# Row softmax on one core: nine load tiles beginning with 13 rows instead of ten beginning with 3 and 5, and every early load on one queue

## The chip, the core and the metric

The kernel runs on one core of a Trainium2 chip. The metric is the device time of one execution in microseconds (us); lower is better. The kernel before was run ten times; the median of those runs is 159.91 us, the lowest 159.77 and the highest 168.56.

## The reference

The input is `x` of shape 16 x 1024 x 512 in fp32, that is, 16,384 rows of 512 numbers. Each row is divided by a temperature of 2 and put through a softmax:

```python
def reference(x):
    x_scaled = x / 2.0
    x_max = np.max(x_scaled, axis=-1, keepdims=True)
    exp_x = np.exp(x_scaled - x_max)
    return (exp_x / np.sum(exp_x, axis=-1, keepdims=True)).astype(np.float32)
```

The input has 33.55 MB and so has the output. Both cross between the main memory (HBM) and the core's own memory (SBUF) once, 67.11 MB in all.

## The kernel before, in words

**Rows.** With 128 partitions, the 16,384 rows make 128 rows for each partition. From here on a "row" is one such step: 128 x 512 numbers, 256 KB, 2 KB in each partition. The kernel takes the exponential of `0.5 * x` without subtracting the maximum. At the end it looks whether all row sums lie in a safe interval, and has a slow general version of the computation (`rounds`) that runs only if they don't. With this input it is skipped.

**Tiles.** `TILES` lists the transfers: how many rows each one moves, and at which row of the buffer `arena` it stands. A tile is one load and, later, one store. In partition p, the rows of a tile lie one after the other both in HBM and in SBUF, so a tile of 15 rows is 128 runs of 30,720 bytes. The buffer has 98 rows (`ARENA`). The first 98 rows of the input are loaded without waiting for anything; the last two tiles, of 15 rows each, are loaded over tiles that have already been stored. `LATE` says which stores each of the two has to wait for.

**Queues.** `early()` issues the first loads ahead of the barrier with which the program begins: tile 0 on SP's queue and tile 1 on ScalarE's. `loads()` issues tiles 2 to 7 on ScalarE's queue (six loads of 15 rows), before ScalarE computes anything. GpSimd issues the two late loads, after the first `TURN` rows (83) have had their exponentials. SP issues all the stores, in the order of the tiles, each as soon as the tile's last multiplication has ended. `SPREAD` names the one tile whose load is cut in three: all rows but the last for 128 partitions, the last row for partitions 0 to 125, and the last row for partitions 126 and 127.

**ScalarE** (ACT, lines L204 and L271) takes one row at a time: an exponential in place, with the row's sum on the side in `stats`. A chunk is 3 rows first (`HEAD`), then always 5 rows (`E`). Before each chunk it waits until the tile that holds it has landed as a whole. TensorE's queue does that waiting: it waits for each tile's `ld` semaphore and then grants that tile's chunks through `s_go` (L140 is the place where ScalarE takes a grant).

**VectorE** (DVE, lines L166 and L169) takes up to three chunks of a tile at a time: a reciprocal of the sums, and one multiplication of up to 15 rows by them. In the last tile it takes one chunk at a time.

The order of the instructions on each engine is written out by hand; no scheduler moves them.

Of the kernel before, what the change touches and what calls it, by code (L numbers as in the profile page):

```python
# [7 lines left out]


TILES = [  # L10
    (3, 0), (5, 3), (15, 8), (15, 23), (15, 38), (15, 53), (15, 68), (15, 83), (15, 0), (15, 15),
]

LATE = {8: (0, 1, 2), 9: (3,)}
ARENA = 98

HEAD = [3]
E = 5

SPREAD = 1  # L20

TURN = 83

LO, HI = 1.0, 1.0e30
G = 64
# [3 lines left out]
def kernel(  # L29
# [5 lines left out]
    nc = tc.nc  # L35
# [24 lines left out]
    tiles, base = [], 0  # L60
# [5 lines left out]
    def dram(ap, t):  # L66
        b, r, _ = tiles[t]
        return ap[b * P : (b + r) * P].rearrange("(p r) d -> p r d", r=r)

    def sb(t):  # L70
        _, r, at = tiles[t]
        return arena[:, at : at + r, :]
# [8 lines left out]

    pairs = []
    for k, t in enumerate(owner):
        most = 1 if t == len(tiles) - 1 else 3
        if pairs and len(pairs[-1]) < most and owner[pairs[-1][0]] == t:
            pairs[-1].append(k)
        else:
            pairs.append([k])
    upto = [1 + max(j for j, ks in enumerate(pairs) if owner[ks[0]] == t) for t in range(len(tiles))]

    ld = [nc.alloc_semaphore(f"ld{t}") for t in range(len(tiles))]
    s_home = {t: nc.alloc_semaphore(f"s_home{t}") for t in LATE}
    s_near = nc.alloc_semaphore("s_near")
# [19 lines left out]
    def load(eng, t):  # L113
        r = tiles[t][1]
        parts = [(0, P, 0, r)]
        if t == SPREAD:
            parts = [(0, P, 0, r - 1), (0, 126, r - 1, r), (126, P, r - 1, r)]
        for p, q, lo, hi in parts:
            eng.dma_start(  # L119
                out=sb(t)[p:q, lo:hi], in_=dram(xf, t)[p:q, lo:hi]  # L120
            ).then_inc(ld[t], 16)

    stored_by = {u: s_home[t] for t, us in LATE.items() for u in us}
    for t, (_, r, at) in enumerate(tiles):
        over = {u for u, (_, ru, au) in enumerate(tiles[:t]) if at < au + ru and au < at + r}
        assert over <= {u for v, us in LATE.items() if v <= t for u in us}

    def landings(ts):
        return 16 * len(list(ts))
# [21 lines left out]
            eng.reg_add(i, i, 1)  # L151

    def early():
        load(nc.sync, 0)
        load(nc.scalar, 1)

    def loads():
        for t in range(2, min(LATE)):
            load(nc.scalar, t)

    def program():
# [13 lines left out]
        nc.gpsimd.memset(ones[:, :], 1.0).then_inc(s_ones, 1)  # L175
        nc.gpsimd.wait_ge(s_exp, starts.index(TURN))
        for t, us in LATE.items():
            nc.gpsimd.wait_ge(s_home[t], landings(us))
# [14 lines left out]
        for t in range(len(tiles)):  # L193
            nc.tensor.wait_ge(ld[t], 48 if t == SPREAD else 16).then_inc(s_go, owner.count(t))
        nc.tensor.wait_ge(s_ones, 1)
# [85 lines left out]
    entry.instructions = []  # L281
    nc.switch_bb("main", None)
    early()
    first = list(entry.instructions)
    at = next(k for k, i in enumerate(head) if type(i).__name__ == "InstDrain")
    entry.instructions = head[:at] + first + head[at:]
    act = []
    entry.instructions = list(entry.instructions) + [i for i in jumps if i not in act]
    nc.switch_body(here, parent=None, valid_engines=[i.engine for i in jumps])
    loads()  # L290
    program()

# [29 lines left out]
```

## Time and profile before

| | before |
|---|---|
| median of ten runs | 159.91 us |
| the profiled execution: its time | 160.02 us |
| the profiled execution: its span, first to last instruction | 158.7 us |
| outside the span in that execution | 1.3 us |
| VectorE busy | 73.2 us, 46% |
| ScalarE busy | 80.6 us, 51% |
| DMA engines, all queues together | 99.0% of 16 engines' span |
| bytes moved | 67.11 MB, 423 GB/s over the span |
| DMA packets | 3024 |

The span is cut into 40 slices of 3.97 us on the profile's page. The row "DMA" gives how busy the core's 16 DMA engines were in each slice, in tenths. The part on DMA queues gives the share of the 16 engines' span that each queue's packets took: q1 is SP's queue (all stores, and the load of tile 0), q10 is ScalarE's (the loads of tiles 1 to 7) and q0 is GpSimd's (the two late loads). A packet here is the run of one tile in one partition: of 30,720 bytes for a tile of 15 rows. With each DMA go 16 tiny packets that raise its semaphore.

### The profile page before, as it was taken

How to read it: one execution, taken by the hardware profiler on the slowest of the kernel's cores; microseconds unless marked ns; L12 is line 12 of the kernel's file. 1: busy time of each engine (PE TensorE's matmuls, PEld its weight loads, DVE VectorE, ACT ScalarE, POOL GpSimd, SP SyncE). 2: the span in 40 equal slices, each digit the busy share in tenths (PEclk: the TensorE clock that was granted, in tenths of full speed). 3: DMA queues.
4: the chain of work that ended last, by engine and by line, in shares of the span. 5: the costliest groups of instructions: out<-in, count | busy, mean ns of one | idle time of the engine just before them, and what ended most of it. 6: DMA issues, size and time to landing. Idle time of an engine off the chain costs nothing. (4 is left out here: it accounts for less than half of the span.)

```text
span 158.7 us, 657 instructions
## 1 busy us (share of the span) xinstructions
PE 0.2 (0%) x2; PEld 0.1 (0%) x2; DVE 73.2 (46%) x27; ACT 80.6 (51%) x257; POOL 2.2 (1%) x8
## 2 busy tenths in 40 slices
PE   0000000000000000000000000000000000000000
PEld 0000000000000000000000000000000000000000
DVE  0047001992981990059500991008922990993000
ACT  0590598696498009940399001991597009940000
POOL 0000000000000000000000300000000000010000
DMA  7999998989899999999999999999999998989895
GB/s 266 386 496 397 463 414 340 511 354 514 387 472 395 472 395 465 403 465 403 457 410 457 410 449 418 441 426 441 426 418 449 418 449 387 480 387 480 387 472 256
DMA packets 3024, 67.11 MB, mean 423 GB/s; under 512 B 336, under 2 KB 336, under 8 KB 720
## 3 DMA queue, kind: packets, MB, share of 16 engines
q1 hardware_dynamic: 1584, 34.34, 50.5%
q10 hardware_dynamic: 1152, 24.90, 37.0%
q0 software_dynamic: 288, 7.86, 11.5%
HBM read 33.55 MB, written 33.55 MB: 423 GB/s over the span
## 5 line engine op out<-in xcount | busy, mean ns | idle before, releaser
L271 ACT ACTIVATE arena<-arena x125 | 76.6, 614 | 54.3 <-ACTq L140 54.3
L169 DVE TENSOR_TENSOR arena<-arena,recip 128x7680 f32<-128x7680 f32 (+2 forms) x12 | 70.2, 5847 | 0.4
L166 DVE RECIPROCAL recip<-stats 128x15 f32<-128x15 f32 (+2 forms) x12 | 2.7, 224 | 70.4 <-ACT arena L271 61.4
L271 ACT ACTIVATION_READ_ACCUMULATOR arena<-arena x125 | 23.4, 187 | 0.0
L200 ACT ACT_TABLE_LOAD x1 | 1.3, 1283 | 5.7 <-issue 5.7
L119 POOL DMA_DIRECT2D arena<-in_x_dram x2 | 1.3, 638 | 84.8 <-ACT arena L271 84.8
L204 ACT ACTIVATE arena<-arena 128x512 f32<-128x512 f32 x3 | 1.9, 618 | 0.0
L180 POOL TENSOR_SCALAR inside<-stats 128x128 f32<-128x128 f32 x1 | 0.6, 631 | 51.8 <-ACT arena L271 51.8
L204 ACT ACTIVATION_READ_ACCUMULATOR arena<-arena 128x1 f32 x3 | 0.6, 186 | 0.0
L196 PE MATMUL total<-ones,count 128*1 128x1 f32 x2 | 0.2, 164 | 143.9 <-DVE inside L184 143.9
L184 DVE SCALAR_TENSOR_TENSOR inside<-inside,stats 128x128 f32<-128x128 f32 x1 | 0.3, 285 | 0.0
L188 DVE TENSOR_SCALAR flag<-total 1x1 int32<-1x1 f32 x1 | 0.1, 147 | 0.3 <-PE total L196 0.3
L196 PEld LDWEIGHTS total<-ones,count 128*1 128x1 f32 x2 | 0.1, 80 | 143.9 <-DVE inside L184 143.9
L175 POOL MEMSET ones<- 128x1 f32 x1 | 0.1, 99 | 2.2 <-POOLq L37 2.2
L306 POOL MEMSET const-float32-0.0<- 128x1 f32 x1 | 0.1, 105 | 0.2 <-issue 0.2
L306 POOL MEMSET const-bfloat16-1.0<- 128x1 bf16 x1 | 0.1, 108 | 0.0
L306 POOL MEMSET const-uint8-127<- 128x1 uint8 x1 | 0.1, 107 | 0.0
L306 POOL MEMSET const-float32-1.0<- 128x1 f32 x1 | 0.1, 105 | 0.0
L184 DVE DVE_READ_ACCUMULATOR inside<-inside,stats 128x1 f32 x1 | 0.1, 83 | 0.0
## 6 DMA issues: line engine op xcount, KB each, us to landing
out_dram<-arena SPq DMA_DIRECT2D x8, 3840.0 KB, 26.3
arena<-in_x_dram ACTq DMA_DIRECT2D x6, 3840.0 KB, 46.7
arena<-in_x_dram POOLq DMA_DIRECT2D x2, 3840.0 KB, 33.7
out_dram<-arena SPq DMA_DIRECT2D x1, 1280.0 KB, 22.8
arena<-in_x_dram ACTq DMA_DIRECT2D x1, 1024.0 KB
arena<-in_x_dram SPq DMA_DIRECT2D x1, 768.0 KB, 5.6
out_dram<-arena SPq DMA_DIRECT2D x1, 768.0 KB, 14.7
arena<-in_x_dram ACTq DMA_DIRECT2D x1, 252.0 KB
```

Of the source, the lines that this page charges most:

```text
L119: eng.dma_start(out=sb(t)[p:q, lo:hi], in_=dram(xf, t)[p:q, lo:hi]).then_inc(ld[t], 16)
L166: nc.vector.reciprocal(out=recip[:, b : b + c], in_=stats[:, b : b + c])._wait_ge(s_exp, ks[-1] + 1).then_inc(s_rec, 1)
L169: nc.vector.tensor_mul(out=arena[:, a : a + c], in0=arena[:, a : a + c], in1=recip[:, b : b + c].unsqueeze(2).to_broadcast([P, c, D]),)._w ...
L175: nc.gpsimd.memset(ones[:, :], 1.0).then_inc(s_ones, 1)
L180: nc.gpsimd.tensor_scalar(out=inside[:, :], in0=stats[:, :], scalar1=LO, scalar2=HI, op0=Alu.max, op1=Alu.min,)._wait_ge(s_exp, len(sizes) ...
L184: nc.vector.scalar_tensor_tensor(out=inside[:, :], in0=inside[:, :], scalar=1.0, in1=stats[:, :], op0=Alu.mult, op1=Alu.is_equal, accum_ou ...
L188: nc.vector.tensor_scalar(out=flag[:, :], in0=total[:, :], scalar1=float(N), scalar2=None, op0=Alu.is_ge,)._wait_ge(s_tot, 1).then_inc(s_f ...
L196: nc.tensor.matmul(total[:, :], lhsT=count[:, :], rhs=ones[:, :], start=True, stop=True)._wait_ge(s_cnt, 2).then_inc(s_tot, 1)
L200: nc.scalar.preload_act_table(Exp)
L204: ins = nc.scalar.activation(out=arena[:, b], in_=arena[:, b], func=Exp, scale=0.5, accum_out=stats[:, b : b + 1],)
L271: ins = nc.scalar.activation(out=data, in_=data, func=Exp, scale=0.5, accum_out=stats[:, r : n_rows - E + 1 + r][:, bass.ds(now, 1)],)
L306: nc = _bacc.Bacc("TRN2", target_bir_lowering=False, num_devices=1)
```

## The change

The list of tiles begins with one of 13 rows where there were one of 3 and one of 5; five of 15 follow, then one of 10, and the two late ones of 15 as before. There are nine tiles for ten. The buffer is filled by the first seven: 13 + 5 x 15 + 10 = 98. The first late tile now lies over tiles 0 and 1, the second over tile 2. The load of tile 0 is the one cut in three (12 rows, then the thirteenth in two pieces), and it is issued by ScalarE; SP issues no load any more. GpSimd waits for 78 rows' exponentials, no longer for 83. VectorE takes one chunk at a time in tile 0 too, so that it multiplies 3, 5 and 5 rows there. The chunks of ScalarE stay as they were.

```diff
 TILES = [
-    (3, 0), (5, 3), (15, 8), (15, 23), (15, 38), (15, 53), (15, 68), (15, 83), (15, 0), (15, 15),
+    (13, 0), (15, 13), (15, 28), (15, 43), (15, 58), (15, 73), (10, 88), (15, 0), (15, 15),
 ]
-LATE = {8: (0, 1, 2), 9: (3,)}
+LATE = {7: (0, 1), 8: (2,)}
 ...
-SPREAD = 1
+SPREAD = 0
-TURN = 83
+TURN = 78
 ...
-        most = 1 if t == len(tiles) - 1 else 3
+        most = 1 if t in (0, len(tiles) - 1) else 3
 ...
     def early():
-        load(nc.sync, 0)
-        load(nc.scalar, 1)
+        load(nc.scalar, 0)
     def loads():
-        for t in range(2, min(LATE)):
+        for t in range(1, min(LATE)):
             load(nc.scalar, t)
```

## Prediction

> **What bounds the kernel now.** I read the page's slices and its DMA queues first. Slices, and then the queues (packets, MB, share of 16 engines' span):
>
> ```profile
> DMA  7999998989899999999999999999999998989895
> DMA packets 3024, 67.11 MB, mean 423 GB/s; under 512 B 336, under 2 KB 336, under 8 KB 720
> q1 hardware_dynamic: 1584, 34.34, 50.5%
> q10 hardware_dynamic: 1152, 24.90, 37.0%
> q0 software_dynamic: 288, 7.86, 11.5%
> ```
>
> Only the first and the last slice are below 8. The shares add up to 99.0%, or 157.1 us of 158.7. The DMA engines bound the kernel. The cleanest price is q0's: two tiles of 15 rows in 11.5% of 158.7 = 18.25 us, so **0.608 us a row**. All 256 rows (128 in, 128 out) cost 155.7 us; 157.1 - 155.7 = 1.4 us is packets that took longer than that.
>
> Then the same by stretches (last columns: DMA share, GB/s), to see where time is lost:
>
> ```profile
> 0.00:1.00 1.00, 0.00 (x0) 0.00 (x0) 0.00 (x0) 0.00 (x0) 0.21 (x4) 1.00 0.00 0
> 1.00:2.00 1.00, 0.00 (x0) 0.00 (x0) 0.00 (x0) 0.00 (x0) 0.00 (x0) 1.00 0.96 258
> 2.00:4.00 2.00, 0.00 (x0) 0.00 (x0) 0.00 (x0) 0.00 (x0) 0.10 (x1) 1.00 0.98 399
> ...
> 24.00:28.00 4.00, 0.00 (x0) 0.00 (x0) 0.87 (x2) 3.06 (x11) 0.00 (x0) 1.00 0.84 333
> 28.00:92.00 64.00, 0.00 (x0) 0.00 (x0) 37.41 (x9) 37.17 (x120) 1.27 (x2) 1.00 1.01 437
> ...
> 157.00:158.70 1.70, 0.00 (x0) 0.00 (x0) 0.00 (x0) 0.00 (x0) 0.00 (x0) 1.00 0.05 18
> ```
>
> Nothing moves for 1.0 us; then there is a ramp; from 28 us on the engines are full to the end. What can be won or lost is at the start, between 2 and 28 us, and at the end if stores run out. The trace's records of single packets size the losses: 0.5 us in the ramp (an engine's first 6 KB packet takes about 0.57 us, later ones 0.23), 0.12 from 2 to 6 us, 0.3 from 6 to 8 us (the first 30 KB packets, behind 2 KB ones, take 1.5 us instead of 1.14), 0.1 near 14 us, 0.23 from 24 to 28 us.
>
> Third, the timeline, for what starts transfers:
>
> ```profile
> 0.00 0.38 SPq L119 DMA_DIRECT2D arena<-in_x_dram  x1
> 0.13 5.51 ACTq L119 DMA_DIRECT2D arena<-in_x_dram  x9
> 17.77 0.63 ACT L271 ACTIVATE arena<-arena  x1 [5.80 <-ACTq L140]
> 27.38 8.16 DVE L169 TENSOR_TENSOR arena<-arena,recip 128x7680 f32<-128x7680 f32 x1
> 87.59 1.27 POOL L119 DMA_DIRECT2D arena<-in_x_dram  x2 [84.84 <-ACT arena L271]
> 130.54 13.49 SPq L137 DMA_DIRECT2D out_dram<-arena  x2
> ```
>
> ScalarE and VectorE wait for loads. The last store is issued at 143.7 us, where the chain of waits ends. All bytes have moved at 158.1. A tile alone takes 15 x 0.608 = 9.1 us, so the last store begins to move at about 149 and lies behind another until then: its issue is not on the path.
>
> **What the Trainium skill says.** "DMA: Bandwidth & Descriptors", section Bandwidth, gives 435 GB/s as the ceiling of the 16 ports. The trace agrees: 432 to 437 GB/s in long stretches. The same page, section Issuing engines are not separate DMA queues, says that starting transfers from several engines saves only the time to start them; that fits SP and ACT sharing the engines here. Its section Queues, rings and completion order says that an engine takes turns between queues packet by packet; loads and stores of 30 KB do share evenly here (tiles land 18.2 us apart, twice 9.1). "Perfetto Trace Analysis", section DMA Instruction — HWDGE (DVE, Sync), says that one block makes the descriptors for both issuing sequencers, so ACT's first load may have stood behind SP's there too; no record here tells that from a wait in the engines, and alone ACT would have neither.
>
> **The change part by part.**
>
> *Queue of the first load.* SP's load goes; the first is ACT's, which began 0.13 us later: **+0.13 us** in device time (in the span it may not show, as that begins with the first instruction). Before, the packet records have SP's first packet at 1.00 us and ACT's only at 2.49. I take it that ACT's queue waited behind packets already fetched: one 0.57 plus four of 0.23 is 1.5 us, just the gap. Stores show the same: the first is issued at 10.94 and moves at 14.98, about three 1.14 us packets late; GpSimd's load is issued at 87.59 and moves at 92.79. So ACT alone should start 1.0 us after its issue. If the delay is ACT's own, it costs 1.36 us more, and then the whole kernel is late by that; kept for the range. Below nothing it can't go by more than those 0.13 us. ACT's nine issues (5.51 us) stay nine; its table load and first exponential follow them, under the load of tile 0.
>
> *Packets.* Before, 10 loads and 10 stores; after, 9 and 9. Each has 128 packets, the tile in three pieces 128 more, each semaphore 16 (32 for that tile): 1280 + 1152 + 304 = 2736 for 3024, or 18 less per engine. The records give 84 ns for 2,048 bytes and 1,138 for 30,720; a straight line leaves 8.7 ns per packet. 18 x 8.7 = **-0.16 us**.
>
> *Start of the loads.* The ramp (0.5 us) stays: each engine still has a first packet. With 24 KB packets the 0.12 us from 2 to 6 should go: **-0.12 us** (0 to -0.12). The one-row pieces still precede 30 KB packets: their 0.3 us stays, moved to about 9 us (I take 0, bounds +0.1 and -0.3).
>
> *Stores begin later.* At 24 to 28 us the store queue passes from 6 KB to 10 KB packets; after, from 26 KB to 30 KB. Before, at 37 to 39 us, the step from 10 KB to 30 KB cost nothing, so I take half of the 0.23 us off: **-0.10 us** (0 to -0.23).
>
> That stores begin later costs nothing by itself, while loads fill the engines. When? Tile 0 lands after 1.9 us (start and losses) + 13 x 0.608 = 9.8, say 10.2 with its semaphore; ScalarE begins 0.7 later (before: landed 17.10 by the records, begins 17.77), takes 13 x 0.615 = 8.0, and VectorE's last 5 rows with their reciprocal 3.1 more. Store 0 is issued at 22.0 instead of 10.9 and 15.1. Its packets move 4 us later, about 25.7. Loads have then moved (25.7 - 1.9) / 0.608 = 39 of 98 rows, so the load queue, fed by about 6 us, doesn't run dry. The cover is there.
>
> *VectorE* gets one more pair, reciprocal 0.2 and the fixed part of a multiplication; it is 46% busy and waits for ScalarE: nothing. ScalarE's 26 chunks stay: nothing.
>
> *The end.* Is the last store still covered? From 25.7 on loads and stores alternate, 1.216 us a row; the load of row 88 (tile 5) lands at 25.7 + 49 x 1.216 - 1.2 (store 0's smaller packets) = 84.1. The 78th row's chunk ends 0.7 + 3.1 later, 87.9; GpSimd's loads move 5.2 later, 93.1. Meanwhile the 10-row tile goes in 20 KB packets, a pair with a store 1.14 + 0.76 = 1.90 us: 4.7 of its 8 done. The other 3.3 share in three, 3.04 us each, to 103.1. Of the late loads' 16 packets 12.7 are left, at 2.28: 132.0. Landing lags, 132.5 to 133. From landing to the last store's issue took 130.57 to 143.69 = 13.1 us; so issue at about **145.8** (before 143.7), first packet from 146.8. The store ahead of it ends 9.1 us before the last byte, at 148.5. Slack falls from about 3.7 to 1.7 us but remains: **0**. Each packet by which the 10-row tile is further on when GpSimd's loads come in takes 1.1 us of it.
>
> *Sum:* +0.13 - 0.16 - 0.12 - 0.10 = **-0.25 us**, 159.77 for the profiled execution of 160.02 us (span 158.7 + 1.3 outside). The median is 0.11 below that one: **159.66 us**.
>
> **The rivals.**
>
> *ScalarE's queue starts late* (slower). For it: its first packet came 2.36 us after its issue, SP's 1.0 after. Against: the shared engines explain that gap. It gives 159.66 + 1.36 = 161.0, and decides from 0.5 us of own delay.
>
> *The last store loses its cover* (slower). If the last tile lands 1.7 us later than worked out, each further us is lost at the end: a slip of two packets gives +0.5, 160.2; of three +1.7, 161.4. Against: the bound on the packet count is about one either way.
>
> *Small packets cost more than I take* (faster). For it: all of the stretched time from 2 to 8 us (0.42) and 24 to 28 us (0.23) stands where 2 to 10 KB packets run. If all goes: +0.13 - 0.16 - 0.42 - 0.23 = -0.68, 159.2.
>
> That tile sizes and queue are without any effect is the forecast's own edge, since it moves little.
>
> **How the numbers follow.** About 0.2% (0.32 us) is what a measurement can tell from no change; -0.25 lies just inside it. The forecast's case gets 0.60, its own range 159.4 to 160.0 (faster 0.29, same 0.27, slower 0.04). ScalarE's late start gets 0.16 and the lost cover 0.10, both slower but for 0.01. Small packets get 0.14 (faster 0.10, same 0.04). That makes faster 0.39, same 0.32, slower 0.29. The range runs from 159.2, the fast rival, to 161.1, past the late start.
>
> **What would show it.** Right: 2736 packets; DMA moving 1.0 us after the first instruction; a full row of nines; the first store issued near 22 us, GpSimd's loads near 88, the last store near 146, the end near 158.4. Wrong: no packets before 2.3 us (late start); a slice below 8 near 147 (lost cover); the first slices no fuller than before (packets didn't matter).

## The result, and the profile after

The changed kernel takes **160.46 us** (median of 9 runs, 160.21 to 160.94); the kernel before 159.87 us. The ratio is 1.0039, with a 95% interval of 1.0030 to 1.0047: 0.59 us slower at the medians. In 4 of its 31 runs the kernel before took 168.2 to 168.9 us, a slower state that all medians and intervals from here on leave out (with it the median is the 159.91 us of the table above). The forecast was 0.25 us faster. The traced executions stand at 160.36 and 160.02 us, with spans of 159.0 and 158.7 us; between them the difference is 0.34 us.

The profile page of the changed kernel, slices and queues as before:

```profile
DMA  8999989899998989899999999999999999999995
DMA packets 2736, 67.11 MB, mean 422 GB/s; under 512 B 304, under 2 KB 304, under 8 KB 432
q1 hardware_dynamic: 1296, 33.56, 48.9%
q10 hardware_dynamic: 1152, 25.69, 38.6%
q0 software_dynamic: 288, 7.86, 11.5%
```

The packets are the 2736 that were counted out. The row is not the full row of nines that was named as a sign of being right: six slices have an 8, as six had before; a packet counts in the slice in which it begins. The shares add up to 99.0% again, and no slice near 147 us is below 9. So the kernel is still bound by the DMA engines, and its end has not lost its cover. The timeline of the changed kernel (start, duration, what):

```profile
0.13 5.50 ACTq L119 DMA_DIRECT2D arena<-in_x_dram  x9
11.49 0.63 ACT L203 ACTIVATE arena<-arena 128x512 f32<-128x512 f32 x1 [4.55 <-ACTq L140]
22.67 0.38 SPq L137 DMA_DIRECT2D out_dram<-arena  x1
90.28 1.27 POOL L119 DMA_DIRECT2D arena<-in_x_dram  x2 [87.53 <-ACT arena L270]
133.42 13.03 SPq L137 DMA_DIRECT2D out_dram<-arena  x2
```

The first store is issued at 22.67 us (22.0 worked out), GpSimd's loads at 90.3 (87.9), the last store at 146.1 (145.8). The mechanics went much as drawn. And once the pipeline runs, both kernels run alike; this is one long stretch in each, the kernel before first (last columns: DMA share, GB/s):

```profile
40.00:150.00 110.00, 0.19 (x2) 0.09 (x2) 58.38 (x20) 55.74 (x180) 1.90 (x3) 1.00 1.00 433
```

```profile
40.00:150.00 110.00, 0.19 (x2) 0.09 (x2) 57.15 (x21) 55.06 (x178) 1.90 (x3) 1.00 1.00 432
```

The difference must lie in the first 40 us, or in how evenly the 16 engines end. Short stretches of this view can't tell it: 16 packets of 30 KB are 0.49 MB, more than 1 us, and are counted whole. The records of single packets can. An undisturbed packet takes 8.7 ns plus 36.8 ns per 1,000 bytes (the straight line of the prediction). "Lost" below is the time gone by, less what the bytes moved in it should have taken, averaged over the engines; the column "to 4 us" begins at the first packet. A few hundredths, also below zero, are the fit's error.

```
us lost:        before first packet | to 4 us | 4-12 | 12-40 | last engine's end
before                 1.00         |  0.58   | 0.39 |  0.24 |  158.15
after                  1.15         |  0.79   | 0.40 |  0.51 |  158.54
after_again            1.14         |  0.85   | 0.55 |  0.03 |  158.51
a_store3_10            1.15         |  0.94   | 0.59 | -0.03 |  158.61
a_store355             1.14         |  0.96   | 0.71 |  0.01 |  159.18
a_3sp_5_5              1.00         |  0.57   | 0.29 |  0.40 |  158.09
```

The third kernel is the changed one, traced again; the last three are experiments below. From the first two rows: +0.15 before the first packet, +0.21 up to 4 us, +0.01 and +0.27 after that, and by the straight line -0.16 for 18 fewer packets on each engine; smaller differences later, -0.09 in all, make it the measured +0.39 at the last packet.

The packets themselves show the start. The first 16 take 0.50 us on average in the kernel before, where one of 6 KB takes 0.23 undisturbed: 0.26 too long. In the changed kernel they take 1.47 us, where one of 24 KB should take 0.91: 0.55 too long.

### The profile page after: what moved, and what is told of

The parts are those of the page before. It is cut to its first block, busy times and chain, and to the rows that moved or that the text cites. A ratio compares the mean times of both kernels' runs of the same rounds, so it can differ in the third digit from the quotient of the medians.

```text
span 159.0 us, 656 instructions
## 1 busy us (share of the span) xinstructions
PE 0.2 (0%) x2; PEld 0.1 (0%) x2; DVE 73.5 (46%) x29; ACT 80.6 (51%) x257; POOL 2.2 (1%) x8
## 2 busy tenths in 40 slices
DMA packets 2736, 67.11 MB, mean 422 GB/s; under 512 B 304, under 2 KB 304, under 8 KB 432
## 3 DMA queue, kind: packets, MB, share of 16 engines
q0 software_dynamic: 288, 7.86, 11.5%
## 5 line engine op out<-in xcount | busy, mean ns | idle before, releaser
L168 DVE TENSOR_TENSOR arena<-arena,recip 128x7680 f32<-128x7680 f32 (+3 forms) x13 | 70.3, 5409 | 0.4
L165 DVE RECIPROCAL recip<-stats 128x15 f32<-128x15 f32 (+3 forms) x13 | 2.8, 219 | 72.5 <-ACT arena L270 59.0
```

The costliest lines, as they stand in the source:

```text
L165: nc.vector.reciprocal(out=recip[:, b : b + c], in_=stats[:, b : b + c])._wait_ge(s_exp, ks[-1] + 1).then_inc(s_rec, 1)
L168: nc.vector.tensor_mul(out=arena[:, a : a + c], in0=arena[:, a : a + c], in1=recip[:, b : b + c].unsqueeze(2).to_broadcast([P, c, D]),)._w ...
```

## The experiments

In all diffs `-` is the kernel that the run starts from: names with a_ start from the changed kernel, names with b_ from the kernel before. Times are medians, with the interval of the ratio to the kernel before. The diffs leave out lines that only follow from those shown or from the text below them (`LATE`, `SPREAD`, the range of a loop, how many semaphore steps are waited for).

**Queue alone, put back (a_sp).**

```diff
-        load(nc.scalar, 0)
+        load(nc.sync, 0)
```

> The changed kernel with one thing put back: tile 0's load is issued by SP instead of ScalarE. Theory (three losses: a later start of 0.15 us, a dearer ramp of 0.2 us because the first packets are 24 KB, a dearer start of the stores of 0.3 us because the first stored packets are 26 KB; against them 0.16 us saved on packets): only the first loss goes, first packet at 1.00 us instead of 1.15, time 160.46 - 0.15 = 160.3. Rival (the queue is the whole difference): time back at 159.9.

160.30 us, 1.0015 to 1.0036; first packet at 1.00 us. The time is the theory's, and the queue is not the whole. But the interval overlaps the changed kernel's, and more than the queue's start changed: tile 0's one-row pieces now took turns with 30 KB packets of the other queue, from 13.6 to 26.5 us by the records, and landed late. The loss near 10 us was gone and a larger one stood between 12 and 40 us; from the first packet to 40 us it came to 1.6 us, as in the changed kernel (1.4 to 1.7). So the 0.15 is not shown cleanly here. Timeline of a_sp:

```profile
28.38 0.63 ACT L203 ACTIVATE arena<-arena 128x512 f32<-128x512 f32 x1 [21.86 <-ACTq L140]
39.55 0.38 SPq L137 DMA_DIRECT2D out_dram<-arena  x1
```

ScalarE began 17 us later than in the changed kernel, and the first store went out 17 us later, yet the time did not rise. No cost of a late start of computing and storing is to be seen here.

**First packets small (a_cut3).**

```diff
-            parts = [(0, P, 0, r - 1), (0, 126, r - 1, r), (126, P, r - 1, r)]
+            parts = [(0, P, 0, 3), (0, P, 3, r - 1), (0, 126, r - 1, r), (126, P, r - 1, r)]
```

> The changed kernel with the first piece of tile 0's load cut in two: 3 rows (6 KB packets), then 9 rows; still on ScalarE's queue, still landing as one tile. Theory (an engine's very first packet is stretched in proportion to its size): the ramp loses 0.2 us less, time about 160.25. Rival (the first bytes cost a fixed delay whatever the packet's size): the ramp stays, the added 128 packets cost 0.07 us, time 160.5.

160.57 us, 1.0031 to 1.0060. The time is the rival's, but it decides nothing: ScalarE issues ten loads here, and that alone turns out below to bring 0.24 us outside the span; with it the theory's 160.25 would be 160.49. The median span is 159.0 us, the changed kernel's 159.2. The trace speaks more clearly. Between the first packet and 4 us it lost 0.83, like the changed kernel, and the first 16 packets took 0.76 us for 0.23: they were 0.52 too long, much as the packets of 24 KB were (0.55). So by this trace it isn't the size of the first packets as such: these had 6 KB, but lay 26 KB apart in HBM.

**First stored packets small, at the same moment (a_store3_10).**

```diff
+CUTS = [(3, 0, 3), (3, 3, 13)]      # multiplications to wait for, first row, end
-        eng.wait_ge(s_mul, upto[t])
-        eng.dma_start(out=dram(of, t), in_=sb(t)).then_inc(sem_of.get(t, s_end), 16)
+        pieces = CUTS if t == 0 else [(upto[t], 0, tiles[t][1])]
+        for n, lo, hi in pieces:
+            eng.wait_ge(s_mul, n)
+            eng.dma_start(out=dram(of, t)[:, lo:hi], in_=sb(t)[:, lo:hi]).then_inc(sem_of.get(t, s_end), 16)
```

> The changed kernel with tile 0 stored in two pieces, 3 rows and then 10, both issued where the one store was issued (22.7 us): only the size of the first stored packets changes, 6 KB instead of 26 KB. Theory (the size of the first stored packets sets what the start of the stores costs): of the 0.54 us lost between 24 and 32 us about 0.3 goes, time about 160.2. Rival (the start of the stores costs the same whatever its size, or depends on when it happens): 160.5.

160.51 us, 1.0031 to 1.0058: no gain in time. In the trace the loss from 12 to 40 us was gone (-0.03 for 0.51), but more was lost up to 12 us, where the two kernels' instructions don't differ.

**Stores held back (b_hold).**

```diff
-        eng.wait_ge(s_mul, upto[t])
+        eng.wait_ge(s_mul, upto[max(t, 1)])
```

> The kernel before with the store of tile 0 held until tile 1's multiplications have ended too (issue at 15.1 us instead of 10.9), so that the stores start later but with 6 KB packets as before. Theory (size, not time): no change, 159.9. Rival (a later start of the stores costs time by itself, half the way to the changed kernel's 22.7 us): about 160.1.

160.09 us, 1.0005 to 1.0029, from 159.78 to 160.57. Slower by between 0.1 and 0.5 us: this is the rival's number, and by the theory it should have been equal. The runs spread more than those of the kernel before, and the one traced is the fastest of them (159.78), so no trace shows where the time went. That a later start of the stores can cost time stays possible.

**Queue alone on the kernel before (b_act).**

```diff
-        load(nc.sync, 0)
+        load(nc.scalar, 0)
```

> The kernel before with one thing changed: tile 0's load is issued by ScalarE, ahead of tile 1's, instead of SP. Theory (the queue costs its later start alone): first packet at 1.15 us instead of 1.00, time 159.9 + 0.15 = 160.05, and up to 4 us the DMA engines lose 1.7 us instead of 1.6. Rival (two queues in the first microseconds fill the engines better than one, so that the queue brings the dearer ramp too): they lose about 1.9 us up to 4 us, time 160.3.

160.27 us, 1.0016 to 1.0035. That is the rival's time, but not by its mechanism: up to 4 us it lost 0.54 after the first packet, as the kernel before does, and its median span is 158.7 for 158.5 us. The other 0.23 us lies outside the span: time less span is 1.58 us for 1.35.

**The same with two loads ahead of the barrier (b_act2).**

```diff
     def early():
-        load(nc.sync, 0)
-        load(nc.scalar, 1)
+        load(nc.scalar, 0)
+        load(nc.scalar, 1, slice(0, 1))      # its 4 rows
     def loads():
+        load(nc.scalar, 1, slice(1, 3))      # its one-row pieces
```

> As b_act (the kernel before with tile 0's load issued by ScalarE), but the two one-row pieces of tile 1 are issued after the opening barrier, so that ScalarE issues two loads ahead of it instead of four; the order on its queue is the same. Theory: b_act's 0.39 us was the later start (0.15) and 0.22 us that lies outside the span and comes with a fourth issue ahead of the barrier; then the time outside the span is back at 1.3 us and the time is 160.05. Rival (one queue in place of two costs the 0.39 by itself): 160.27 again.

160.32 us, 1.0013 to 1.0037; outside the span still 1.60. The place ahead of the barrier is not the reason. What b_act, b_act2 and a_cut3 (1.54 outside) share is ten loads on ScalarE's queue; all kernels with nine or fewer have 1.28 to 1.37.

**Ten loads alone (b_10loads)**, and **nine where there were ten (a_9loads)**, the latter against a_3sp_5_5 below:

```diff
+        if t == 7:
+            parts = [(0, P, 0, 8), (0, P, 8, r)]
```

> The kernel before with tile 7's load issued by ScalarE as two (8 rows and 7 rows), so that ScalarE issues ten loads, not nine; tile 7 lands far from the start and the end. Theory (ten loads bring about 0.25 us outside the span): 1.6 us outside, span 158.5, time 160.1. Rival (they don't): 159.9.

```diff
-        for t in range(2, min(LATE)):
+        load(nc.sync, 2)
+        for t in range(3, min(LATE)):
             load(nc.scalar, t)
```

> a_3sp_5_5 with tile 2 (5 rows) loaded by SP after the barrier, so that ScalarE issues nine loads, not ten. Theory (ten loads on ScalarE's queue bring about 0.25 us outside the span; all four kernels with ten have 1.54 to 1.60 us there, all others 1.30 to 1.37): the time outside the span is back at 1.3 us, the span stays near 158.5, time 159.9: all of the change but its first tile and queue is then free. Rival (the time outside the span has another cause): 160.1 again.

b_10loads: 1.59 us outside the span, as expected, but 162.89 us in all (1.0178 to 1.0225), its span at 161.3: the split of tile 7 cost 2.8 us of its own, which is not explained, so the 158.5 expected of the span was missed. a_9loads: 1.36 outside, as expected, but 160.14 us (1.0011 to 1.0036), the time of its rival: the span is 158.8, 0.3 more than expected, which SP's load may have brought; that is not shown. That a tenth load on ScalarE's queue brings about 0.24 us outside the span is shown from both sides; what does it is not. The changed kernel has nine, so this is no part of its 0.59.

**The head of the kernel before on the changed one (a_3sp_10, then a_3sp_5_5).**

```diff
-    (13, 0), (15, 13), ...
+    (3, 0), (10, 3), (15, 13), ...              # a_3sp_10
+    (3, 0), (5, 3), (5, 8), (15, 13), ...       # a_3sp_5_5
-        load(nc.scalar, 0)
+        load(nc.sync, 0)
+        load(nc.scalar, 1)
```

> The changed kernel with its first tile replaced by two, 3 rows issued by SP and 10 rows issued by ScalarE (the second one cut for its last row), so that it begins as the kernel before does; all later tiles, the 10-row tile and GpSimd's 78 rows stay as changed. Theory (all that was lost lies in how the transfers begin): time back at 159.9. Rival (the later tiles, the 10-row tile or the end of the stores cost something): at least 160.1.

> The changed kernel with its first tile replaced by three: 3 rows issued by SP, 5 and 5 by ScalarE, the second one cut for its last row: the start is exactly that of the kernel before, and the later tiles (five of 15, one of 10, two of 15), GpSimd's 78 rows and the smaller multiplications at the start are those of the change. Theory (the loss lies in the first packets read and the first packets stored): 159.9 to 160.0. Rival (the later tiles carry what a_3sp_10 still lost): 160.2.

a_3sp_10: 160.24 us, 1.0017 to 1.0034, from 159.96 to 160.91: it misses the theory's 159.9 and gets back about 0.2 of the 0.59 us. a_3sp_5_5: 160.14 us, 1.0010 to 1.0024, between theory and rival, but with ten loads, so 1.59 us outside; **its span is 158.5 us, the same as before**, in 19 runs. By the span, the five later tiles of 15, the 10-row tile, GpSimd's 78 rows and the small multiplications cost nothing, and all that the change loses is in its first tile (as it is loaded and as it is stored) and that tile's queue. In time this stays unconfirmed: a_9loads, which was to show it without the tenth load, reached 160.14 us and not 159.9.

**No one-row pieces (a_nospread), or ahead of the others (a_order, b_order), or in a later tile (b_spread5).**

```diff
-SPREAD = 0
+SPREAD = -1                                                        # a_nospread
-            parts = [(0, P, 0, r - 1), (0, 126, r - 1, r), (126, P, r - 1, r)]
+            parts = [(0, 126, r - 1, r), (126, P, r - 1, r), (0, P, 0, r - 1)]   # a_order, b_order
-SPREAD = 1
+SPREAD = 5                                                         # b_spread5
```

> The changed kernel with tile 0 loaded by one DMA, not in three pieces: no one-row packets, and each of the 16 DMA engines gets the same bytes. Theory: the 0.36 us lost near 10 us, where 30 KB packets follow the 2 KB ones, goes; two engines that now end 0.5 to 1.1 us ahead of the others move as much as they do: time about 160.1. Rival (that loss is only the step from one DMA to the next, or the unequal pieces make up for engines that start late): 160.5 or more.

160.63 us, 1.0031 to 1.0056. The rival's time came. The loss near 10 us went (-0.02 for 0.36 from 8 to 12 us), but two engines ended at 158.9 and 159.0 us, the next at 158.3. The two one-row pieces come with 16 semaphore packets together, where every other transfer has 16 of its own (304 in all); read as 14 for 126 partitions and 2 for two, this leaves out two engines when the larger piece is loaded and spares them some eight packets of 84 ns, 0.67 us. That is about what the last two are now late by; that they are the same two is inferred, since the records don't name the engine.

> The changed kernel with the one-row pieces of tile 0 issued ahead of its 12 rows instead of behind. The bytes for each DMA engine stay unequal as before. Theory (2 KB packets cost 0.36 us where 30 KB packets follow and nothing else is queued; a_nospread lost that gain again because it made the engines' shares equal): the loss near 10 us goes, time about 160.1. Rival (the loss moves to the place where the 24 KB packets follow the 2 KB ones): 160.46.

> The kernel before with the one-row pieces of tile 1 issued ahead of its 4 rows, where SP's packets of tile 0 are still queued beside them. Theory: the 0.36 us lost between 6 and 8 us goes and nothing takes its place, time about 159.55, under both kernels. Rival (the first 30 KB packets cost that whatever precedes them): 159.88.

162.62 us (1.0161 to 1.0189) and 160.99 us (1.0060 to 1.0085). Both theories fail, and both times lie above the rivals' too: with the pieces first, a_order lost 1.33 us up to 4 us after its first packet, and b_order 0.87 from 4 to 8 us.

> The kernel before with the cut into three pieces moved from tile 1 to tile 5, which is loaded while stores run. Theory (a 2 KB packet ahead of a 30 KB one costs only where no other queue has packets to fill in): the 0.36 us lost between 6 and 8 us goes, time about 159.6, under both kernels. Rival (the loss is that of the first 30 KB packets whatever precedes them): 159.9.

164.04 us, 1.0212 to 1.0289. This run shows the rival of the prediction that the change did not meet, a lost cover. Lines of b_spread5: ScalarE's wait for tile 5 (timeline), SP's stores (timeline), the end (stretches):

```profile
72.19 0.63 ACT L271 ACTIVATE arena<-arena  x1 [20.89 <-ACTq L140]
```

```profile
10.87 142.06 SPq L137 DMA_DIRECT2D out_dram<-arena  x10
```

```profile
150.00:154.00 4.00, 0.19 (x2) 0.09 (x2) 2.93 (x4) 0.00 (x0) 0.22 (x1) 1.00 0.32 138
154.00:158.00 4.00, 0.00 (x0) 0.00 (x0) 0.00 (x0) 0.00 (x0) 0.00 (x0) 1.00 0.87 369
```

The one-row pieces took turns with stores, tile 5 landed late, everything behind it slipped, and the last store was issued at about 152.6 us (143.7 before). The DMA engines, idle for two thirds of 150 to 154 us, waited for it.

**Start of the stores: early and small on the changed kernel (a_store355), late and large on the kernel before (b_store2first).**

```diff
+CUTS = [(1, 0, 3), (2, 3, 8), (3, 8, 13)]               # a_store355, used as in a_store3_10
-        for t in range(len(tiles)):                      # b_store2first
+        for t in (2, 0, 1, *range(3, len(tiles))):
             store(nc.sync, t)
```

> The changed kernel, loads untouched, but tile 0 stored in three pieces of 3, 5 and 5 rows, each as soon as its rows are multiplied (first store at about 15.5 us, 6 KB packets first, as in the kernel before). Theory A (the start of the stores is half of the 0.4 us that the large first tile costs): time 160.2. Theory B (all of it is the start of the loads): 160.5, a little more for the added packets.

> The kernel before, loads untouched, but tile 2 (15 rows) is stored ahead of tiles 0 and 1, so that the stores start at about 35.6 us and with 30 KB packets. Theory A (large first stored packets cost about 0.2 us): 160.1. Theory B (only the start of the loads counts): 159.9.

a_store355: 160.93 us (1.0041 to 1.0084), slower than either theory. The loss from 12 to 40 us is down to 0.01, but more than that is lost up to 12 us, with the same loads, and one engine ended 0.4 us behind the rest. b_store2first: 160.67 us (1.0031 to 1.0077). From 36 to 40 us, where its 30 KB stores begin, it lost 0.54, against 0.24 in all from 12 to 40 us before; another 0.46 is lost between 80 and 100 us. So a late and large start of the stores can cost on the kernel before; an early and small one on the changed kernel brings no time back.

**Both kernels traced again (after_again, before_again).** No edit.

> The changed kernel once more, for a second trace of it. Theory (the start of the loads with 13 rows is dearer and varies from execution to execution: 1.2 us lost between the first packet and 12 us in its first trace, 1.5 and 1.7 in two traces of kernels with the same loads): between 1.15 and 1.7 us. Rival (1.2 is what it always costs, and the other two have it from their stores): 1.15 to 1.25 us.

> The kernel before once more, for a second trace. Theory: between the first packet and 12 us it loses 0.9 to 1.05 us, as in all traces of kernels with its first tiles, and 0.2 to 0.3 between 12 and 40 us. Rival (it varies as much as the changed kernel): outside one of these.

after_again, 160.33 us: between the first packet and 12 us it lost 1.41 us, against 1.19 in the first trace, so this varies. From 12 to 40 us it lost 0.03 for 0.51, so that varies too, and the last packet came at the same time within 0.03 us. before_again lost 0.98 up to 12 us (0.97 in the first trace) and 0.13 from 12 to 40 us, below what was expected; its execution was disturbed later by one DMA engine that ended 7.4 us after the others, so nothing after 40 us is used.

Put together, the loss up to 4 us after the first packet is 0.54 to 0.60 us in the eleven traces whose first tile has 3 rows and whose second has 4 or 5 (before, before_again, b_hold, b_act, b_act2, b_spread5, b_order, b_10loads, b_store2first, a_3sp_5_5, a_9loads), 0.70 in a_3sp_10, and 0.79 to 0.97 in the seven with a first tile of 13 (a_order, with its pieces ahead, apart). The first 16 packets are 0.12 to 0.29 us too long in these twelve, 0.49 to 0.76 in these seven. Where the rest is lost varies from trace to trace, but from the first packet to 40 us the sum keeps the two groups apart: 1.4 to 1.7 us in the seven, 0.9 to 1.3 in ten of the twelve (b_order and b_store2first, which change the order of the pieces or of the stores, have 1.8 and 1.5). The means are 1.6 and 1.2.

## Why the prediction was wrong, point by point

- **The bound, the cover, the mechanics: right.** DMA engines full to the end, packet count 2736, issues of stores and late loads within 0.3 to 2.4 us of those worked out, no loss at the end. That the last store came within 0.3 us is in part luck: GpSimd's loads were issued 2.4 us late and their first packet moved at 95.0 us for 93.1, and this was made up later, when the stores paused (95.5 to 98.0 and 116.0 to 117.3 us by the packet records) and the loads ran alone.
- **Queue: right.** +0.13 was put; the first packet came 0.15 later, 1.0 us after ScalarE's issue. The rival of ScalarE's own delay is out. That the span might not show it was wrong: other instructions still begin at 0.
- **Packets: the count was right.** 2736, so 18 fewer per engine. The -0.16 is the straight line's price for them; no run measures it by itself.
- **Start of the loads: this step failed, in sign.** I let the ramp stay at its 0.5 us, because each engine still has one first packet, and put -0.12 us beside it, between 0 and -0.12, taking the stretched packets for a cost of small packets. It is +0.21 and +0.27 up to 4 us in the two traces, and +0.01 and +0.16 more by 12 us: in the first traces the opening packets of the 13-row tile are stretched by 0.55 us, those of the 3-row tile by 0.26. The small first tile of 3 rows was the cheap way to begin. The bounds let in no loss, though nothing in the trace excluded one: no trace of the kernel before shows a large first tile.
- **Start of the stores: not confirmed.** I put -0.10, between 0 and -0.23; the two traces have +0.27 and -0.21 from 12 to 40 us. This term varies from execution to execution, as does how evenly the engines end, and no run here pins its mean.
- **The sum.** With the first trace: 0.15 + 0.21 + 0.01 + 0.27 - 0.16 - 0.09 = 0.39 at the last packet. The means of the two groups say about the same: 1.6 - 1.2 = 0.4 us up to 40 us, where -0.22 was put, with +0.15 and -0.16 beside it. The medians of the time differ by 0.59, of which the traced executions hold 0.34; the traced one of before lay 0.15 above its median and that of after 0.10 below.
- **The forecast's case** was given 159.4 to 160.0; 160.46 lies between it and the late start (161.0). A lost cover of two to three packets would have given such a time (160.2 to 161.4), but the cover held; so the outer range, to 161.1, holds the number by no case that the prediction had named.

What stays open: why a large first tile begins dearer. a_cut3 speaks against packet size, and for the distance of the first reads in HBM (6 KB packets 26 KB apart lost 0.78 us up to 2.5 us and were 0.52 too long at first; b_act's, 6 KB apart, lost 0.56 and were 0.24 too long; both on ScalarE's queue). That is one trace each, no run changes the distance alone, and so it is argued, not shown.

None of the versions tried beats the kernel before.

## What to carry to other kernels

In this kernel, whose DMA engines are full from end to end, the sizes of the later tiles cost nothing that the span shows. Starting to compute 17 us later cost nothing visible in a_sp, but b_hold and b_store2first, in which the stores of the kernel before begin later, came out slower, so a late start is not always free. What counted was the first microseconds and that the last store is issued in time. Where a kernel is like this one, try first a small transfer whose rows lie close together, from the queue that is ready first, even if larger packets cost less in the long run. When a term of a sum can't be read from the trace, bound it on both sides of zero: "small packets cost more" was a guess about a cause, and it set the sign.

## What the runs showed of the hardware that was not expected

- A tenth load on ScalarE's queue came with about 0.24 us outside the span (1.54 to 1.60 us in five kernels with ten, 1.28 to 1.37 in the others).
- Packets of 2 KB that took turns with 30 KB packets of another queue let a small piece land very late: tile 0 of a_sp was waited for until 28.4 us, for 11.5 in the changed kernel.
- The same loads lost 1.19, 1.41, 1.53 and 1.68 us between the first packet and 12 us in four traces (after, after_again, a_store3_10, a_store355), while nine of the eleven with the small first tile (b_order and b_spread5 move the one-row pieces) stayed between 0.86 and 1.12: the start with the large first tile is less steady, and the kernel's times spread by 0.7 us instead of 0.4 (though a_3sp_10, with the small tile, spreads by 0.95). How much of it shows by 12 us depends on the one-row pieces: a_sp and a_nospread, also with 13 rows, lost only 0.97 and 0.94 up to there, and more than the others between 12 and 40 us (0.6 and 0.7).
